# Norms of six attention heads and three SSD groups by sums in rows, a factor row that goes through DRAM, and a third weight set added up by GpSimd

## The chip, the cores and the metric

The kernel runs on one core of a Trainium2 chip. The metric is the device time of one execution in microseconds (us). A core has a matrix engine (TensorE, "PE" in the profile, its weight loads "PEld"), an elementwise engine (VectorE, "DVE"), an activation engine (ScalarE, "ACT"), a third elementwise engine (GpSimd, "POOL"), and SP, which only issues DMAs. Each engine works through its own list of instructions in order; semaphores hold an instruction back until what it reads is there.

## The reference

One layer of a hybrid decoder on 512 tokens of width 1024: a SwiGLU feed-forward part (FFN1), a mixer in which a Mamba-2 state-space part (SSD, 16 heads in 4 groups) and a differential attention (8 heads of width 128) share the input and the output projection, a cross-attention into 256 memory tokens, a second feed-forward part (FFN2), and norms before each. The two places whose norms the change touches:

```python
y = y.reshape(bsz, seqlen, SSD_WIDTH) * jax.nn.silu(z.astype(jnp.float32))
yg = y.reshape(bsz, seqlen, SSD_GROUPS, SSD_WIDTH // SSD_GROUPS)
yg = yg * lax.rsqrt(jnp.mean(yg * yg, axis=-1, keepdims=True) + EPS)
...
o = diff_attention(q, k, v, lam, rel_bias)
o = o * lax.rsqrt(jnp.mean(o * o, axis=-1, keepdims=True) + EPS)
y_attn = (o.astype(h.dtype) * subln_w * (1.0 - lambda_init)).reshape(bsz, seqlen, DA_WIDTH)
...
return jnp.concatenate([y_ssd, y_attn], axis=-1) @ w_out
```

Each attention head is normed over its 128 columns, each SSD group over its 256.

## The kernel before

Activations lie with the channel on the 128 partitions and the 512 tokens along the free axis, so a head's output `po` or half a group's output `y` is one 128x512 tile. Every fp32 product is done in three fp32r passes: an operand is split into a high part (`hi`, a rounded copy by ScalarE) and a low part (`lo`, the rest, a subtraction by VectorE), and high x high, high x low and low x high are added up in PSUM (`split`, `split_w`, `weights`, `proj`). Weights come by SP's DMA queue into `wr` tiles (six buffers), their two parts into `wh` and `wl` (three buffers each).

FFN1 and FFN2 save products in the manner of Strassen and Winograd: blocks of weights and of activations are added up first (`sums_in_steps` for the activations, sums `S1` to `S4`), and seven products stand in for eight. `out_blocks` is FFN's output product: `oa` = B11 x "11", `oe` = S1 x S1, `ob` = a copy of `oa` plus S2 x S2, then B21, S3, S4 and "22". `parts` are its two pairs of weight blocks. FFN1's last third runs it with `by_dma=True`: the sums of weights are made there, S1 and S3 by fetches that add on arrival (from GpSimd's DMA queue, `added`), S2 (the third set of weights, from `t_raw`) by adds of VectorE (`t2`, line 1366) of the blocks `more` that `ask_early` fetched. The generator stops once (`yield` behind `ready`), before the last activations are gated, and goes on when the products start.

The order of TensorE's work is written by a planner at build time. `Order` has a list of dense work (projections) and chains beside it (heads, groups, norms); a chain's `yield d` means "not before d us more of planned TensorE time", and while it waits the dense work is issued. The table `W` holds these times. On SP and GpSimd the written order stands; on the other engines the scheduler may move an instruction within its dependences, and `behind(...)` orders it.

A head (`head`): scores, softmax, transposes, `po`; then ScalarE copies `po` to `of`, four transposes to `ptk` put tokens on partitions, ScalarE squares them with an accumulator (`ss`), VectorE makes `ev`, GpSimd the power -1/2 (`rr`, line 858), VectorE multiplies (`on`, line 860), four transposes to `pot` turn it back, and the split into `ya` takes the gain `wsub` with it. `out_attn(0, ...)` and `out_attn(1, ...)` multiply heads 0 to 3 and 4 to 7 by their output weights (`pm`), and wait at build time until all four `ya` are there.

A group (`group`): at the end the two halves `yz` are squared and added, four products with a column of ones give the sums per token (`pn`), GpSimd takes the power, and `row_of` turns the factors into a row: two diagonal matrices `ndiag` (by GpSimd in groups 0 to 2, by VectorE in group 3), two products with ones (`nrow`); VectorE multiplies (line 1034) and `ys` is split. `out_proj` needs `ys` 0 to 5 first, and the last two (group 3) later.

All along, `block_sums_in_dram` adds up FFN2's weight blocks in DRAM: one fetch by SP and one accumulating DMA by GpSimd for each, of 512 KB mostly.

Of the kernel before, what the change touches and what calls it, by code (L numbers as in the profile page):

```python
# [11 lines left out]
F32 = mybir.dt.float32  # L12
# [5 lines left out]
P = 128  # L18
# [82 lines left out]
def body(tc, a, dbg=None):  # L101
# [25 lines left out]
    def small(s, n, bufs=None):  # L127
        return tiny.tile([P, n], F32, tag=s, name=nm(s), bufs=bufs)
# [15 lines left out]
    def mm(out, w, x, start, stop):  # L144
        od.t += (1 if w.dtype == R32 else 4) * (x.free_size() + 8) / 2400
        newest_mm[:] = [nc.tensor.matmul(out, w, x, start=start, stop=stop).ins]  # L146

    def transpose(out, x):
        od.t += 2 * (P + 8) / 2400
        nc.tensor.transpose(out, x, ident)  # L150
# [617 lines left out]
    def head(hd, q, kq, bias):  # L768
# [73 lines left out]
        w0.clear()  # L842
        w1.clear()
        of = s2("of")
        S.activation(of, po, AF.Copy)
# [8 lines left out]
        ev = small("ev", 4)  # L854
        V.scalar_tensor_tensor(ev, sm[0], EPS, sm[0], ALU.mult, ALU.mult)
        V.scalar_tensor_tensor(ev, ss, 1.0 / P, ev, ALU.mult, ALU.add)  # L856
        rr = small("rr", 4)
        G.tensor_tensor(rr, ev, mhalf, ALU.pow)  # L858
        on = s2("on", shape=(P, 4, P))
        V.tensor_tensor(on, pt.rearrange("p (a b) -> p a b", b=P), rr[:, :, None].to_broadcast([P, 4, P]), ALU.mult)  # L860
        yield W["hp"]
        pt = aux("pot")
        for b in range(4):
            transpose(pt[:, b * P : (b + 1) * P], on[:, b])
        ya[hd] = split("ya", backwards(pt), wsub)
        dump(f"ya_{hd}", ya[hd][0])

    wcv = []

# [60 lines left out]
    def group(g, bt, ct, xs, zs):  # L930
# [93 lines left out]
        yield W["gq"] + (1.2 if g == 2 else 0.0)  # L1024
        pn = aux("pn", (P, 4))
        for b in range(4):
            mm(pn[:, b : b + 1], sq[0][:, b * P : (b + 1) * P], ones[:, 0:1], True, True)

        rh = inv_rms_cols(pn, 4, 4.0 / (4 * 256), 4.0 * EPS)
        yield W["gn"]  # L1030
        pr = yield from row_of(rh, 4, *((G, G) if g < 3 else (V, V)), W["gr"] - (0.8 if g == 3 else 0.0))
        for j in range(2):
            n = 2 * g + j
            V.scalar_tensor_tensor(yz[j], yz[j], par[:, C_SSD + n : C_SSD + n + 1], pr, ALU.mult, ALU.mult)
            ys[n] = split("ys", yz[j])
            dump(f"ys_{n}", ys[n][0])


# [254 lines left out]
    def out_blocks(blocks, sums, g, col4, ncol4, each=None, finale=None, clean=True, n=None, by_dma=False):  # L1293
# [11 lines left out]
            nc.sync.dma_start(raw, of[:, part[0] * T : part[1] * T])  # L1305
            return raw

        def weights(of, part, raw=None, low_behind=()):
# [5 lines left out]
            high = S.activation(hi, raw, AF.Copy)  # L1314
            with behind(low_behind):
                low = V.tensor_tensor(lo, raw, hi.bitcast(F32), ALU.subtract)  # L1316
            recent[:] = [high.ins, low.ins]
            return hi, lo

        def some(ps, w, which, part, t, first, ks=None, passes=range(3)):  # L1320
# [39 lines left out]
            return t_raw[part]  # L1360

        def t2(part):
            more = pieces.pop(part) if part in pieces else (fetch(blocks[B22], part),)
            n = t_raw[part].shape[1] // len(more)
            for i, m in enumerate(more):
                V.tensor_tensor(t_raw[part][:, i * n : (i + 1) * n], t_raw[part][:, i * n : (i + 1) * n], m, ALU.add)
            return t_raw[part]

        def b21(part):
# [9 lines left out]
        later, pieces, asked = {}, {}, {}  # L1379

        def ask_early():
            for of, make in ((B11, lambda part: fetch(blocks[B11], part)), (S1, t1)):
                asked[of, parts[1]] = make(parts[1])
            for part in parts:
                pieces[part] = [s2("more") for _ in range(*part)]
                for k, m in zip(range(*part), pieces[part]):
                    nc.sync.dma_start(m, blocks[B22][:, k * T : (k + 1) * T])
# [28 lines left out]
        for m in both:  # L1416
            yield from m
        u2 = []
        third = {part: weights(sums[2], part, low_behind=() if n else sums_low) for n, part in enumerate(parts if by_dma else parts[:1])}
        third_split = list(recent) if by_dma else []  # L1420
        for t in range(2):
            S.activation(b_ps[t], a_ps[t], AF.Copy)
# [202 lines left out]
```

## Time and profile before

| | |
|---|---|
| median of 3 runs | 1295.64 us (1294.69 to 1296.42) |
| the profiled execution | 1296.8 us, span 1295.0 us |
| mean granted TensorE clock | 0.996 |
| POOL, busy | 116.4 us (9%) |
| DMA | 234.75 MB, mean 181 GB/s |

The span goes from the first to the last instruction; the time of an execution has a little more around it. A row of the chain of waits or of the timeline is "start us, us, engine, what". A group is "line engine operation out<-in, shapes xcount | busy us, mean ns | idle before, and what ended it". The stage in question of FFN1 lies from 300 to 343 us, the heads and groups from 385 to 805, FFN2 from 960 on.

### The profile page before, as it was taken

How to read it: one execution, taken by the hardware profiler on the slowest of the kernel's cores; microseconds unless marked ns; L12 is line 12 of the kernel's file. 1: busy time of each engine (PE TensorE's matmuls, PEld its weight loads, DVE VectorE, ACT ScalarE, POOL GpSimd, SP SyncE). 2: the span in 40 equal slices, each digit the busy share in tenths (PEclk: the TensorE clock that was granted, in tenths of full speed). 3: DMA queues.
4: the chain of work that ended last, by engine and by line, in shares of the span. 5: the costliest groups of instructions: out<-in, count | busy, mean ns of one | idle time of the engine just before them, and what ended most of it. 6: DMA issues, size and time to landing. Idle time of an engine off the chain costs nothing.

```text
span 1295.0 us, 20087 instructions
## 1 busy us (share of the span) xinstructions
PE 1282.7 (99%) x7709; PEld 1124.9 (87%) x7709; DVE 973.5 (75%) x1553; ACT 707.2 (55%) x1203; POOL 116.4 (9%) x145
## 2 busy tenths in 40 slices
PE   9999999999999999999999999999999999999997
PEld 7889998998888788877888888889899999989995
DVE  6988898797875776567778697645678878877886
ACT  7545564565654564346644575435466646555554
POOL 1001010001010011100102011020001000000000
PEclk9999999999999999999999999999999999999998
DMA  9368677889874436653475667593249876666662
GB/s 334 97 175 205 181 204 196 226 200 238 260 242 147 139 66 164 225 165 98 106 206 168 175 161 232 190 231 111 66 131 253 212 228 178 191 189 189 184 198 91
DMA packets 69551, 234.75 MB, mean 181 GB/s; under 512 B 8192, under 2 KB 9696, under 8 KB 69104
## 3 DMA queue, kind: packets, MB, share of 16 engines
q1 hardware_dynamic: 53488, 180.91, 42.5%
q0 software_dynamic: 13168, 45.67, 20.0%
q10 hardware_dynamic: 2800, 6.91, 1.6%
q8 instruction: 60, 0.98, 0.3%
q14 instruction: 35, 0.29, 0.1%
HBM read 231.30 MB, written 48.29 MB: 216 GB/s over the span
## 4 chain that ended last, share of the span: by engine, by line
PE 98%; DVE 1%; ACT 0%; issue 0%; POOLq 0%; POOL 0%; ACTq 0%
PE qb L243 13%; PE pm L146 10%; PE qe L243 8%; PE qa L243 8%; PE pxbc L146 7%; PE ob L1328 7%; PE oa L1328 4%; PE oe L1328 4%; PE pk L146 3%; PE pv L146 3%; PE pq L146 3%; PE pcq L146 3%; PE pz L146 3%; PE pck L146 2%; PE pa L146 2%; PE pcv L146 2%
## 5 line engine op out<-in xcount | busy, mean ns | idle before, releaser
L155 ACT ACTIVATE wh<-wr 128x1024 fp32r<-128x1024 f32 (+1 forms) x245 | 251.5, 1028 | 239.0 <-PE qe L243 29.4
L156 DVE TENSOR_TENSOR wl<-wr,wh 128x1024 fp32r<-128x1024 f32 (+1 forms) x245 | 291.1, 1189 | 78.3 <-ACT wh L155 57.8
L1314 ACT ACTIVATE wh<-wr 128x1024 fp32r<-128x1024 f32 (+1 forms) x78 | 77.1, 988 | 71.3 <-PE ob L1328 19.7
L1316 DVE TENSOR_TENSOR wl<-wr,wh 128x1024 fp32r<-128x1024 f32 (+1 forms) x78 | 87.6, 1131 | 15.1 <-ACT wh L1314 12.9
L790 ACT ACTIVATE ec<-ec,mn 128x512 f32<-128x512 f32 (+3 forms) x64 | 35.4, 554 | 21.9 <-DVE mn L789 21.9
L789 DVE CUSTOM_DVE_ANT_0 ec<-ps,bias 128x512 f32<-128x512 f32 (+3 forms) x64 | 28.1, 487 | 15.4 <-PE ps L146 15.3
L252 POOL DMA_DIRECT2D wr<-in_f2q x11 | 9.7, 881 | 308.8 <-DMA wr<-in_f2q 176.3
L367 POOL TENSOR_TENSOR ncol<-nv,mhalf 128x4 f32<-128x4 f32 (+1 forms) x9 | 10.6, 1179 | 295.3 <-DVE nv L365 295.3
L903 DVE SCALAR_TENSOR_TENSOR conv<-pxbc,par,conv 128x511 f32<-128x511 f32 (+2 forms) x48 | 35.8, 745 | 0.6
L146 PE MATMUL pxbc<-hnl,wh 128*128 128x512 f32 x128 | 35.5, 404 | 0.0
L146 PE MATMUL pxbc<-hnh,wh 128*128 128x512 f32 x128 | 34.7, 398 | 0.0
L146 PE MATMUL pxbc<-hnh,wl 128*128 128x512 f32 x128 | 32.5, 393 | 0.0
L454 DVE TENSOR_TENSOR gate<-qb,row 128x512 f32<-128x512 f32 x19 | 13.2, 692 | 22.1 <-PE qb L243 22.1
L146 PEld LDWEIGHTS pxbc<-hnh,wl 128*128 128x128 f32 x128 | 23.7, 188 | 5.2 <-issue 0.2
L252 POOL DMA_DIRECT2D wr<-in_f1q x16 | 14.0, 874 | 151.9 <-DMA wr<-in_f1q 83.0
L146 PEld LDWEIGHTS pxbc<-hnh,wh 128*128 128x128 f32 x128 | 23.3, 189 | 4.6 <-issue 0.3
L146 PEld LDWEIGHTS pxbc<-hnl,wh 128*128 128x128 f32 x128 | 23.2, 188 | 4.7 <-issue 0.4
L455 ACT ACTIVATE gate<-gate 128x1024 f32<-128x1024 f32 x19 | 20.1, 1056 | 10.9 <-DVE gate L454 10.9
L146 PE MATMUL pv<-wh,hnh 128*128 128x512 f32 x64 | 25.3, 396 | 0.0
L146 PE MATMUL pv<-wh,hnl 128*128 128x512 f32 x64 | 25.2, 393 | 0.0
L155 ACT ACTIVATE s24h<-s 128x512 fp32r<-128x512 f32 x30 | 18.8, 626 | 8.1 <-DVE s L214 8.1
L858 POOL TENSOR_TENSOR rr<-ev,mhalf 128x4 f32<-128x4 f32 x8 | 8.3, 1035 | 162.4 <-DVE ev L856 162.4
(465 smaller groups left out, 3548.1 us busy)
## 6 DMA issues: line engine op xcount, KB each, us to landing
wr<-in_f2q SPq DMA_DIRECT2D x44, 512.0 KB, 4.5
wr<-in_f1q SPq DMA_DIRECT2D x40, 512.0 KB, 4.6
wr<-in_f1b SPq DMA_DIRECT2D x23, 512.0 KB, 7.0
isum<-in_f2q SPq DMA_DIRECT2D x22, 512.0 KB, 5.2
wr<-isum SPq DMA_DIRECT2D x22, 512.0 KB, 6.2
wsum<-in_f2b SPq DMA_DIRECT2D x20, 512.0 KB, 6.1
wr<-wsum SPq DMA_DIRECT2D x20, 512.0 KB, 4.7
wr<-in_f1q POOLq DMA_DIRECT2D x16, 512.0 KB, 7.6
```

The source lines that it names most:

```text
L146: newest_mm[:] = [nc.tensor.matmul(out, w, x, start=start, stop=stop).ins]
L155: S.activation(hi, src, AF.Copy),
L156: V.tensor_tensor(lo, src, hi.bitcast(F32), ALU.subtract),
L243: newest_mm[:] = [nc.tensor.matmul(out, w_[:, wc], xs[kp][which][x_], start=first and j == 0 and f == 0 and kp == 0, stop=j == 2 and kp == ...
L252: last_sum[:] = [G.dma_start(raw, m, accum_op=ALU.add).ins]
L455: S.activation(gate, gate, AF.Silu)
L789: V.tensor_tensor_reduce(out=ec[:, :n], in0=ps[c][:, parts[i]], in1=bias[:, T - n :], scale=0.125, scalar=3e38, op0=ALU.add, op1=ALU.min, ...
L790: S.activation(ec[:, :n], ec[:, :n], AF.Exp, bias=mn, scale=-1.0, accum_out=sm[c][:, i : i + 1])
L903: V.scalar_tensor_tensor(y[:, d:], ps[:, : T - d], par[:, cw + j : cw + j + 1], y[:, d:], ALU.mult, ALU.add)
L1314: high = S.activation(hi, raw, AF.Copy)
L1316: low = V.tensor_tensor(lo, raw, hi.bitcast(F32), ALU.subtract)
L1328: newest_mm[:] = [nc.tensor.matmul(ps, a_[:, ts], b_[:, ws], start=first and k == 0 and j == 0, stop=k == n - 1 and j == 2, skip_group_che ...
```

## The change

There are three edits. (1) Heads with `hd % 4 < 3`, six of eight: `po` is squared by ScalarE, the squares are split, and two products with ones (`sums_by_token`, `ptok`) put the sum over the channels into every partition; VectorE takes the diagonal of each 128x128 block with `tensor_tensor_reduce`, which gives a column per token. The factors go to DRAM as a column and come back as a row on all partitions (`row_by_dram`, two DMAs of GpSimd), and GpSimd multiplies, copies and subtracts (`times_row`), so that the parts of `ya` need no transposes. Heads 3 and 7 keep the old way (`by_token`). (2) Groups 0 to 2 the same with `ys`; the gain is taken by ScalarE beforehand; group 3 keeps the old way. (3) In FFN1's last third the adds of the third weight set go to GpSimd (`add_pieces`); `ask_early` is called before the stop, S3's fetches are asked for later and part by part, the second part of B11 is split behind the first block's parts (`first_block`), and the third set's high part is made before the products, its low part after them.

```diff
+W |= {"hn": 4.2, "fw": 5.0, "fr": 16.0}
...
+    def sums_by_token(sq):
+
+        ps = aux("ptok")
+        with behind(list(newest_mm)):
+            for j in range(2):
+                mm(ps, ones_r, sq[j], j == 0, j == 1)
+        ss = small("ss", 4)
+        junk = s2("junk", shape=(P, P))
+        for b in range(4):
+            V.tensor_tensor_reduce(out=junk, in0=ps[:, b * P : (b + 1) * P], in1=ident, scale=1.0, scalar=0.0, op0=ALU.mult, op1=ALU.add, accum_out=ss[:, b : b + 1])
+        return ss
+
+    def row_by_dram(col):
+        there = dram.tile([4, P], F32, name=nm("there"))
+        G.dma_start(bass.AP(there.tensor, there.offset, [[1, P], [P, 4]]), col)
+        yield W["fw"]
+        row = s2("far")
+        G.dma_start(row, bass.AP(there.tensor, there.offset, [[0, P], [1, 4 * P]]))
+        yield W["fr"]
+        return row
+
+    def times_row(src, row, seen=lambda t: t):
+
+        hi, lo = s2("farh", R32), s2("farl", R32)
+        G.tensor_tensor(src, src, row, ALU.mult)
+        G.tensor_copy(hi, seen(src))
+        G.tensor_tensor(lo, seen(src), hi.bitcast(F32), ALU.subtract)
+        return hi, lo
...
-        S.activation(of, po, AF.Copy)
-        yield W["hv"]
-        pt = aux("ptk")
+        if hd % 4 < 3:
+            sq = s2("osq")
+            S.activation(sq, po, AF.Square)
+            S.activation(of, po, AF.Copy, scale=wsub)
+            sq = split("osq", sq)
+            yield W["hn"]
+            ss = sums_by_token(sq)
+        else:
+            S.activation(of, po, AF.Copy)
+            yield W["hv"]
+            pt = aux("ptk")
+            ss = by_token(pt, of)
...
+        if hd % 4 < 3:
+            row = yield from row_by_dram(rr)
+            ya[hd] = times_row(of, row, backwards)
...
+        gains = [par[:, C_SSD + 2 * g + j : C_SSD + 2 * g + j + 1] for j in range(2)]
+        if g < 3:
+            sq = split("ysq", sq[0])
+            for j in range(2):
+                S.activation(yz[j], yz[j], AF.Copy, scale=gains[j])
+            yield W["gq"] + (1.2 if g == 2 else 0.0)
+            row = yield from row_by_dram(inv_rms_cols(sums_by_token(sq), 4, 4.0 / (4 * 256), 4.0 * EPS))
...
+            if g < 3:
+                ys[n] = times_row(yz[j], row)
...
         def t2(part):
-            more = pieces.pop(part) if part in pieces else (fetch(blocks[B22], part),)
-            n = t_raw[part].shape[1] // len(more)
-            for i, m in enumerate(more):
-                V.tensor_tensor(t_raw[part][:, i * n : (i + 1) * n], t_raw[part][:, i * n : (i + 1) * n], m, ALU.add)
+            V.tensor_tensor(t_raw[part], t_raw[part], fetch(blocks[B22], part), ALU.add)
             return t_raw[part]
...
-            for part in parts:
-                asked[S3, part] = seventh(part)
+            add_pieces(parts[0])
+
+        def add_pieces(part):
+            for i, more in enumerate(pieces.pop(part)):
+                to = t_raw[part][:, i * T : (i + 1) * T]
+                G.tensor_tensor(to, to, more, ALU.add)
...
             ready = [{parts[0]: weights(of, parts[0])} for of in (blocks[B11], sums[0])]
+            if by_dma:
+                ask_early()
             yield
         if by_dma:
-            ask_early()
+            asked[S3, parts[0]] = seventh(parts[0])
+            ready[0][parts[1]] = weights(None, parts[1], asked.pop((B11, parts[1])), first_block)
+            with behind(first_block[:1]):
+                third[parts[0]] = weights(None, parts[0], t_raw[parts[0]], low=False)
+            copied_behind = [recent[0]]
...
-        third = {part: weights(sums[2], part, low_behind=() if n else sums_low) for n, part in enumerate(parts if by_dma else parts[:1])}
-        third_split = list(recent) if by_dma else []
-        for t in range(2):
-            S.activation(b_ps[t], a_ps[t], AF.Copy)
-        with behind(third_split):
+        if by_dma:
+            V.tensor_tensor(third[parts[0]][1], t_raw[parts[0]], third[parts[0]][0].bitcast(F32), ALU.subtract)
+            add_pieces(parts[1])
+            asked[S3, parts[1]] = seventh(parts[1])
+        else:
+            third[parts[0]] = weights(sums[2], parts[0], low_behind=sums_low)
+        with behind(copied_behind):
+            copied = [S.activation(b_ps[t], a_ps[t], AF.Copy).ins for t in range(2)]
+        if by_dma:
+            with behind(copied):
+                third[parts[1]] = weights(None, parts[1], t_raw[parts[1]])
+        with behind(list(recent) if by_dma else []):
             for t in range(2):
                 update(t + 2, 1, e_ps[t], 1, False)
```

More of the change, by code (lines that the diff above doesn't have):

```diff
@@ L844, in head, with by_token @@
         of = s2("of")
-        S.activation(of, po, AF.Copy)
-        yield W["hv"]
-        pt = aux("ptk")
+        if hd % 4 < 3:
[10 more added lines that the diff above has]
+            ss = by_token(pt, of)
+        ev = small("ev", 4)
+        V.scalar_tensor_tensor(ev, sm[0], EPS, sm[0], ALU.mult, ALU.mult)
+        V.scalar_tensor_tensor(ev, ss, 1.0 / P, ev, ALU.mult, ALU.add)
+        rr = small("rr", 4)
+        G.tensor_tensor(rr, ev, mhalf, ALU.pow)
+        if hd % 4 < 3:
+            row = yield from row_by_dram(rr)
+            ya[hd] = times_row(of, row, backwards)
+        else:
+            on = s2("on", shape=(P, 4, P))
+            V.tensor_tensor(on, pt.rearrange("p (a b) -> p a b", b=P), rr[:, :, None].to_broadcast([P, 4, P]), ALU.mult)
+            yield W["hp"]
+            pt = aux("pot")
+            for b in range(4):
+                transpose(pt[:, b * P : (b + 1) * P], on[:, b])
+            ya[hd] = split("ya", backwards(pt), wsub)
+        dump(f"ya_{hd}", ya[hd][0])
+    def by_token(pt, of):
         for b in range(4):
@@ L853, in head @@
             S.activation(junk, pt[:, b * P : (b + 1) * P], AF.Square, accum_out=ss[:, b : b + 1])
[L854 to L866, printed above, removed]
+        return ss
     wcv = []
@@ L1023, in group @@
         V.tensor_tensor(sq[0], sq[0], sq[1], ALU.add)
[L1024 to L1031, printed above, removed]
+        gains = [par[:, C_SSD + 2 * g + j : C_SSD + 2 * g + j + 1] for j in range(2)]
[5 more added lines that the diff above has]
+            row = yield from row_by_dram(inv_rms_cols(sums_by_token(sq), 4, 4.0 / (4 * 256), 4.0 * EPS))
+        else:
+            yield W["gq"]
+            pn = aux("pn", (P, 4))
+            for b in range(4):
+                mm(pn[:, b : b + 1], sq[0][:, b * P : (b + 1) * P], ones[:, 0:1], True, True)
+            rh = inv_rms_cols(pn, 4, 4.0 / (4 * 256), 4.0 * EPS)
+            yield W["gn"]
+            pr = yield from row_of(rh, 4, V, V, W["gr"] - 0.8)
         for j in range(2):
             n = 2 * g + j
-            V.scalar_tensor_tensor(yz[j], yz[j], par[:, C_SSD + n : C_SSD + n + 1], pr, ALU.mult, ALU.mult)
-            ys[n] = split("ys", yz[j])
+            if g < 3:
+                ys[n] = times_row(yz[j], row)
+            else:
+                V.scalar_tensor_tensor(yz[j], yz[j], gains[j], pr, ALU.mult, ALU.mult)
+                ys[n] = split("ys", yz[j])
             dump(f"ys_{n}", ys[n][0])
@@ L1306, in fetch, with weights @@
             return raw
-        def weights(of, part, raw=None, low_behind=()):
+        def weights(of, part, raw=None, low_behind=(), low=True):
             if raw is None:
@@ L1314, in weights @@
             high = S.activation(hi, raw, AF.Copy)
+            recent[:] = [high.ins]
             with behind(low_behind):
-                low = V.tensor_tensor(lo, raw, hi.bitcast(F32), ALU.subtract)
-            recent[:] = [high.ins, low.ins]
+                if low:
+                    recent.append(V.tensor_tensor(lo, raw, hi.bitcast(F32), ALU.subtract).ins)
             return hi, lo
@@ L1377, in t4 @@
             G.dma_start(t_raw[part], blocks[B21][:, part[0] * T : part[1] * T], accum_op=ALU.add)
-        later, pieces, asked = {}, {}, {}
+        later, pieces, asked, third, copied_behind = {}, {}, {}, {}, []
         def ask_early():
```

1 line of the change is left out of this document (added).

## The prediction

> **What bounds the kernel now.** I read the page first (busy time, chain by engine), then the waits of TensorE, then the timeline and the chain of waits where TensorE waits longest, then the groups of the tiles that the diff removes.
>
> ```profile
> span 1295.0 us, 20087 instructions
> PE 1282.7 (99%) x7709; PEld 1124.9 (87%) x7709; DVE 973.5 (75%) x1553; ACT 707.2 (55%) x1203; POOL 116.4 (9%) x145
> ...
> PE 98%; DVE 1%; ACT 0%; issue 0%; POOLq 0%; POOL 0%; ACTq 0%
> ```
>
> The waits of TensorE and of its weight loads (us in total, times, longest):
>
> ```profile
> PE ob L1328 <- ACT wh L1314: 1.1, 1, 1.1
> ...
> PEld ptk L150 <- ACT of L845: 0.9, 4, 0.3
> ...
> PEld pot L150 <- DVE on L860: 0.4, 2, 0.2
> ...
> PEld oe L1328 <- DVE s31l L156: 0.2, 1, 0.2
> ```
>
> TensorE is busy 99% and is 98% of the chain that ended last. So the end moves for two reasons only: instructions leave TensorE's stream, or one of its few waits goes or comes. After the start-up the longest wait is one in front of `ob`, the S2 product at the end of FFN1. The timeline around it (start, us, what), then the chain of waits, then busy us of TensorE, its weight loads, VectorE, ScalarE and GpSimd in stretches of 1 us, with the granted clock behind them:
>
> ```profile
> 310.27 0.69 DVE L156 TENSOR_TENSOR s24l<-s,s24h 128x512 fp32r<-128x512 f32 x1
> ...
> 310.88 0.69 DVE L156 TENSOR_TENSOR gl<-th,gh 128x512 fp32r<-128x512 f32 x1
> 311.48 2.49 DVE L1366 TENSOR_TENSOR wr<-wr,more 128x512 f32<-128x512 f32 x4
> ...
> 311.82 1.03 PE L146 MATMUL prel<-hot,rel_sb 32*8 32x256 f32 x4
> ...
> 312.86 2.27 ACT L1314 ACTIVATE wh<-wr 128x1024 fp32r<-128x1024 f32 x2 [1.14 <-DVE wr L1366]
> ```
>
> ```profile
> 313.97 7.33 PE ob L1328 x24
> 321.31 5.44 PE oa L1328 x24
> ```
>
> ```profile
> 312.00:313.00 1.00, 0.85 (x4) 0.17 (x2) 1.00 (x3) 0.14 (x1) 0.79 (x1) 1.00 0.99 397
> 313.00:314.00 1.00, 0.03 (x1) 0.03 (x1) 1.00 (x3) 0.92 (x1) 0.00 (x0) 1.00 1.03 406
> ...
> 315.00:316.00 1.00, 1.00 (x3) 0.78 (x3) 1.00 (x2) 1.00 (x5) 0.52 (x1) 0.50 0.98 352
> ```
>
> The third set of weights (S2's) is made last: VectorE finishes the blocks' low parts, only then adds `more` into it, then ScalarE splits it. TensorE idles 0.15 + 0.97 = 1.1 us. Then the granted clock falls to 0.50, and the 24 products take 7.33 us where the next 24 take 5.44: another 1.9 us. The unit price of a 512-column product is 5.44 / 24 = 0.227 us.
>
> The Trainium skill ("TensorE: Matmul & The Clock Gate", What's actually happening) puts the fall to half speed after an idle window of about 3.4 us. Here it followed 1.1 us of idleness behind the four small `prel` products; by that page alone the gap costs 1.1 us and not 3.0, and the sum below would be -5.2 instead of -7.1; the measured clock decides.
>
> **The change, part by part.** *Six heads.* The path of TensorE loses eight 128x128 transposes a head and gets two 512-column products with ones.
>
> ```profile
> 467.32 1.90 PE po L146 x12
> ...
> 470.78 0.44 PE ptk L150 x4
> ...
> 478.18 0.44 PE pot L150 x4
> ...
> 486.96 0.44 PE ptk L150 x4
> ```
>
> That is 0.44 + 0.44 - 2 x 0.227 = 0.43 us a head, 2.6 us for six. The waits of `ptk` and `pot` (0.9 and 0.4 us over eight heads) go with them, about 1.0 for six. In their place the sums wait for a longer line: Square, copy with gain, high part (ScalarE), low part (VectorE), instead of one copy; the plan gives it 4.2 instead of 2.08 us. I cost the old waits and the new ones as equal, 0, between -1.0 (none left) and +1.8 (the longest old one, 0.3, at all six). The scores and transposes of other heads and the dense products stand between, so TensorE waits only for what arrives late.
>
> Behind the sums nothing of these heads is on TensorE: four diagonal products (VectorE), `ev`, the power on GpSimd, a DMA to DRAM, one back to all partitions, and three 128x512 passes on GpSimd.
>
> ```profile
> L858 POOL TENSOR_TENSOR rr<-ev,mhalf 128x4 f32<-128x4 f32 x8 | 8.3, 1035 | 162.4 <-DVE ev L856 162.4
> ...
> L698 POOL TENSOR_TENSOR ea<-euler,hb 128x16 f32<-128x16 f32 x1 | 2.9, 2923 | 6.1 <-DMA hb<-in_hb 6.1
> ...
> L789 DVE CUSTOM_DVE_ANT_0 ec<-ps,bias 128x128 f32<-128x128 f32 x16 | 4.0, 286 | 0.0
> L860 DVE TENSOR_TENSOR on<-ptk,rr x8: 691/692/692, 420.9 to 647.6; 128x512 f32<-128x512 f32 x8
> L160 DVE SCALAR_TENSOR_TENSOR yal<-pot,wsub,yah 128x512 fp32r<-128x512 f32 x8 | 6.0, 748 | 3.7 <-ACT yah L159 3.5
> 385.00:505.00 120.00, 119.97 (x635) 95.77 (x634) 82.12 (x216) 64.49 (x163) 12.29 (x14) 1.00 0.47 123
> ```
>
> VectorE loses `on` and `yal` (0.69 + 0.75) and gets the low part of the squares and four diagonals (0.69 + 4 x 0.29 = 1.83): +0.4 us a head, in a stretch where it is busy 82 of 120 us; hidden. ScalarE, busy 64 of 120, loses four squares with accumulators and a split, and gets two passes. GpSimd gets three passes and two DMA issues, at 12 busy us of 120. Two of the passes read the block backwards, which no row shows on GpSimd; I bound a pass between 0.69 us (VectorE's for a block of that size) and 2.9 (GpSimd's longest, `ea`) and take 1.03, that of `ndiag` (quoted below), the row of equal size and engine.
>
> *Does the row come in time?* Head 2 is the last with the new norm ahead of the output product.
>
> ```profile
> L146 PEld LDWEIGHTS pm<-yah,wh x64: 186/188/190, 504.2 to 763.6; 128*128 128x128 f32 x64
> ...
> cum_d<-ct_sb POOLq DMA_DIRECT2D x1, 32.0 KB, 2.5
> ...
> hb<-in_hb POOLq DMA_DIRECT2D x1, 16.0 KB, 7.0
> ...
> isum<-in_f2q POOLq DMA_DIRECT2D x1, 512.0 KB, 13.7
> ```
>
> Its `po` ends at 469.2; with 4.2 planned the sums run at 473.5 and end at 474; 1.2 (diagonals), 0.3 (`ev`), 1.0 (power) and 0.9 (issue) give 477.4. The first reader of `ya` is at 504.2, the passes take 3.1, so both DMAs together have 504.2 - 3.1 - 477.4 = 23.7 us. I bound one by 2.5 us (the small write of `cum_d`) and 13.7 (the slowest block sum on that queue, since these stand before them in it): 5 to 27 us, and take 2 x 7.0, the small load `hb` on the same queue, the nearest to the broadcast. So 10 us are left: cost 0, and at the upper end 3.7 us late. The 512 scattered words of the write are in no row; the same bounds serve. While GpSimd waits to issue the read, block sums and the next head's power queue behind it. Head 3's `ptk` is at 487.0 and its power comes after, so a write that lands within 10 us of 477.4 delays nobody; one that lands later holds `on` of head 3 and then its `pot`. SP's queue is not passed by any of these; its fetches of block sums merely find their adders later.
>
> *Three groups.* TensorE loses `pn` (four fp32 products) and `nrow`, and gets two products:
>
> ```profile
> 541.78 0.79 PE pn L146 x8
> ...
> 549.31 0.46 PE nrow L146 x2
> L146 PEld LDWEIGHTS pm<-ysh,wh x64: 186/188/189, 793.3 to 834.7; 128*128 128x128 f32 x64
> 756.52 0.79 PE pn L146 x8
> ```
>
> 0.79 + 0.46 - 0.45 = 0.80 us each, 2.4 us for three. The results are needed from 793.3 on; group 2, the last, has its sums at 756.5 and has 36.8 us for 7 us of instructions, 3.1 us of further passes and two DMAs: hidden. Group 3, which really ends late, keeps its old norm.
>
> *The third set.* The adds go to GpSimd, the first part's before the blocks are made, its high part in front of the products, its low part behind them. Then nothing of VectorE's line lies ahead of `ob` except `s24` (ready at 311.0), so up to 1.1 us of idleness and 1.9 us of slow clock go, plus 0.2 that `oe` waits for `s31l` (the last row of the waits above): 3.2 at most.
>
> ```profile
> 294.10 1.75 SPq L1387 DMA_DIRECT2D more<-in_f1b  x4
> ...
> 311.91 0.88 POOL L1354 DMA_DIRECT2D gate<-in_f1b  x1 [6.59 <-ACT ob L1422]
> ```
>
> The fetches that move with it (B11 and S1 of the second part, S1's accumulating one on GpSimd, four `more`) keep their order on SP, which held `more` to 294.1; their earlier place gains and costs 0. On GpSimd the second part's adds now stand before S3's accumulating fetch, issued at 311.9 today. S3 is read after `oa`, at 321.3 + 5.4 = 326.7, or 3 us sooner; 2.1 us of adds leave it 9.7 us. I cost that at 0; at the slowest row, 13.7, it would be 4 us.
>
> Below, the gain is bounded by nothing, and by a loss if the adds hold up VectorE, for which this trace has a row:
>
> ```profile
> 702.81 1.03 POOL L378 TENSOR_TENSOR ndiag<-ident,cl 128x512 fp32r<-128x512 f32 x1
> ...
> 703.05 1.87 DVE L156 TENSOR_TENSOR wl<-wr,wh 128x1024 fp32r<-128x1024 f32 x1 [0.41 <-PE pxbc L146]
> L156 DVE TENSOR_TENSOR wl<-wr,wh 128x1024 fp32r<-128x1024 f32 x229 | 280.1, 1224 | 77.2 <-ACT wh L155 57.8 <-PE pv L146 5.0 <-PE pxbc L146 4.0
> ```
>
> A low part that takes 1.22 us took 1.87 beside the GpSimd pass: 0.65 lost, as if it had started only when that pass ended at 703.84. VectorE is fully busy in all three windows above, and the second part's two adds fall on `s31l` and `s24l`, two-input operations like that one. So I leave about 0.65 of the 1.1 idle us standing, count the 0.2 as kept, and let the clock recover: 0.5 + 1.9 = 2.4 us gained, between -1.3 (two such losses and no gain, slower) and 3.2.
>
> The Trainium skill ("SBUF — State Buffer", two separate sides) makes this a rule: GpSimd and a VectorE operation with two SBUF inputs exclude each other for a whole instruction. The trace agrees with its 1.87 us; by the rule alone the adds free nothing on VectorE, since four passes of 1.03 us lock out more than the 2.5 us that they took there; with the clock's 1.9 us alone left of the third set the sum would be -6.6.
>
> In the mixer 36 such passes come and six `ndiag` passes go. Each burst of three can push one low part by 0.65: 12 bursts, 0 to 7.8 us. Behind 703.05 TensorE did not wait, and VectorE has a third of its time free; I take 0.3.
>
> **The sum**: -2.6 (heads) - 2.4 (groups) - 2.4 (third set) + 0.3 = -7.1 us. The profiled execution took 1296.8 us (1.8 around its span), so 1289.7; the median of the runs, 1295.64, is 1.2 below it: **1288.5 us**.
>
> **Rivals.** (a) *The third set is still what ends last*: its raw part, the copies of `oa` or the locked-out low parts arrive no earlier, the gap and the slow clock stay, and only 2.6 + 2.4 - 0.3 = 4.7 us come: 1290.9. For it: VectorE had no free time there. Against: the high part, the wait that ended last, no longer stands behind VectorE. Here the change would not do what it says.
>
> (b) *The lock reaches TensorE*: every burst costs its 0.65, and the third set gains only 2: -2.6 - 2.4 - 2.0 + 7.8 = +0.8, no change, 1296.4. For it: 703.05. Against: low parts are made a set or more ahead.
>
> (c) *The row comes late, slower than before*: it decides from the point where write and read of heads 2 and 6 take over 23.7 us together. At 13.7 each TensorE waits 3.7 us at both attention output products, and pays 1.9 of slow clock each time: +11.2 - 7.1 = +4.1, 1299.7. For it: the read waits in GpSimd's line, behind block sums in the same queue. Against: 10 us of room.
>
> **How the numbers follow.** Forecast 0.60 (1286 to 1290.5); (a) 0.19 (1290.5 to 1293); (b) 0.12 (1293 to 1298); (c) 0.06; 0.03 for a larger gain, where no new wait takes the place of the 1.0 at the transposes and the third set yields 3.2 (1286 and below). A measurement of this kernel can tell about 0.2% from no change, 2.6 us. Faster by that, under 1293.05: the forecast, (a), the larger gain and a little of (b), 0.83; within it, most of (b): 0.10; slower: (c) and an end of (b): 0.07. The range 1285.3 to 1293.5 takes in the forecast's bounds (1.9 more at best) and (a), and leaves out under 2 in 10.
>
> **What would show it.** Right: in six heads two `ptok` products of some 0.45 us together where eight transposes took 0.88; no clock of 0.50 between 312 and 320 and 5.4 us for `ob`; `pm` not waiting for `ya`. Wrong: a wait of `pm` on GpSimd or a DMA (c); low parts over 1.8 us with TensorE waiting behind them (b); a window at 0.50 still there (a). Waits of the new products for the low part of the squares over 0.3 us would make the heads' step wrong.

## The result, and the profile after

| | before | changed |
|---|---|---|
| median | 1294.69 us (1293.2 to 1296.42, 5 runs) | 1309.11 us (1306.51 to 1310.17, 5 runs) |
| profiled execution, span | 1296.8, 1295.0 us | 1309.11, 1307.3 us |

The ratio is 1.0109, with a 95% interval of 1.0098 to 1.012: slower by 14 us, where 7 us faster was forecast. The page of the changed kernel (span, busy time, chain by engine):

```profile
span 1307.3 us, 20098 instructions
PE 1285.3 (98%) x7649; PEld 1122.9 (86%) x7649; DVE 976.2 (75%) x1606; ACT 703.6 (54%) x1164; POOL 168.4 (13%) x191
PE 93%; DVE 3%; DMA 2%; issue 1%; ACT 1%; POOL 0%; POOLq 0%; DVEq 0%; ACTq 0%
```

60 matmuls have left the stream, yet TensorE is busy longer: it ran part of them at a lower clock. Its waits (us in total, times, longest):

```profile
PE pn L147 <- DVE ysq L1069: 4.4, 1, 4.4
PE ptok L147 <- ACT osqh L156: 4.2, 1, 4.2
PE pf L147 <- DVE st L1024: 1.9, 2, 1.5
...
PE py L147 <- DVE gate L1041: 1.1, 1, 1.1
PE oe L1385 <- DVE s31l L157: 0.9, 1, 0.9
```

Apart from `oe`, they lie in three places, around 625, 735 and 800 us, and the granted clock falls in each (windows of the changed kernel; the number before the two last columns is the clock):

```profile
620.00:625.00 5.00, 2.59 (x14) 1.64 (x12) 0.70 (x2) 0.70 (x2) 3.15 (x4) 1.00 0.31 46
625.00:630.00 5.00, 3.10 (x15) 1.91 (x16) 4.79 (x13) 3.67 (x10) 1.39 (x2) 0.72 0.62 100
630.00:635.00 5.00, 5.00 (x18) 3.93 (x19) 4.97 (x26) 3.36 (x11) 1.87 (x2) 0.59 0.26 69
...
735.00:740.00 5.00, 3.89 (x22) 3.08 (x22) 5.00 (x9) 2.77 (x5) 0.26 (x1) 0.66 1.03 236
...
805.00:810.00 5.00, 4.97 (x12) 3.54 (x13) 1.67 (x4) 0.00 (x0) 4.86 (x6) 0.50 0.71 296
```

**Head 6** (timeline of the changed kernel; in brackets the idle time before and what ended it):

```profile
612.81 0.83 POOL L385 DMA_DIRECT2D there<-rr  x1 [0.96 <-POOL rr L891]
621.68 0.55 POOL L388 DMA_DIRECT2D far<-there  x1 [8.05 <-PE pxbc L147]
622.25 1.28 POOL L395 TENSOR_TENSOR of<-of,far 128x512 f32<-128x512 f32 x1
...
623.56 0.69 DVE L819 CUSTOM_DVE_ANT_0 ec<-ps,bias 128x512 f32<-128x512 f32 x1 [6.62 <-POOL of L395]
...
626.06 0.63 ACT L156 ACTIVATE osqh<-osq 128x512 fp32r<-128x512 f32 x1
...
626.74 0.50 PE L147 MATMUL ptok<-osqh,ones_r 128*128 128x512 f32 x1 [4.15 <-ACT osqh L156]
```

GpSimd issues head 5's write at 612.8 and stands 8 us in front of head 5's read. (By the trace the write lands at 621.1, and the read starts 0.6 us later, as each of the nine reads does behind its write; the releaser named there is that of another semaphore.) Behind the read in its list stands head 4's multiplication, whose row is there. VectorE's `ec` of the next softmax gets the tile that this multiplication gives back, so it waits 6.6 us, ScalarE's squares stand behind it, and TensorE behind those.

**The memory tiles** of the cross-attention come by GpSimd's queue too, and now stand behind group 1's read:

```profile
705.67 0.86 POOL L385 DMA_DIRECT2D there<-ncol  x1 [0.30 <-POOL ncol L368]
...
716.79 0.59 POOL L388 DMA_DIRECT2D far<-there  x1 [9.35 <-DMA there<-ncol]
717.91 3.05 POOL L1100 DMA_DIRECT2D mem<-in_memT  x5
...
729.49 0.51 ACT L160 ACTIVATE hm<-mem,par 128x256 fp32r<-128x256 f32 x1 [5.69 <-DMA mem<-in_memT]
...
731.20 2.31 DVE L157 TENSOR_TENSOR wl<-wr,wh 128x1024 fp32r<-128x1024 f32 x1
...
733.90 0.49 PE L147 MATMUL pf<-th,st 128*128 128x128 f32 x2 [1.46 <-DVE st L1024]
```

Before, these loads were issued from 705.0 on:

```profile
L1044 POOL DMA_DIRECT2D mem<-in_memT x8: 538/1136/1192, 705.0 to 713.2; - x8
```

The low part `wl`, ahead of the `st` that `pf` waits for, takes 2.31 us beside a pass of GpSimd (731.07 to 732.42), where such low parts take 1.22.

**Groups 2 and 3**, ahead of the output projection:

```profile
780.29 0.86 POOL L385 DMA_DIRECT2D there<-ncol  x1 [0.30 <-POOL ncol L368]
...
793.95 0.59 POOL L388 DMA_DIRECT2D far<-there  x1 [12.79 <-PE pcv L147]
...
801.22 2.20 POOL L395 TENSOR_TENSOR y<-y,far 128x512 f32<-128x512 f32 x1 [5.75 <-DMA far<-there]
802.21 1.75 DVE L1069 TENSOR_TENSOR ysq<-ysq,ysq 128x512 f32<-128x512 f32 x1
...
804.11 1.28 PE L147 MATMUL pn<-ones,ysq 128*128 128x1 f32 x8 [4.40 <-DVE ysq L1069]
```

The first `pm` needs group 2's parts, which GpSimd makes from 801 on. Before, eight of these products lay ahead of group 3's `pn`; now nothing is left to run ahead of it. And `ysq`, which `pn` waits for, takes 1.75 us beside GpSimd's pass, where its neighbours of that size take 0.69.

The common part is the write. Issues of the changed kernel (KB each, median us to landing):

```profile
far<-there POOLq DMA_DIRECT2D x9, 256.0 KB, 7.1
...
there<-rr POOLq DMA_DIRECT2D x6, 2.0 KB, 10.1
...
there<-ncol POOLq DMA_DIRECT2D x3, 2.0 KB, 10.9
```

2 KB take over 10 us, longer than the 256 KB of the row, and GpSimd stands in front of all nine reads.

### The profile page after: what moved, and what is told of

It is laid out like the page before. It is cut to its first block, busy times and chain, and to the rows that moved or that the text cites. A ratio compares the mean times of both kernels' runs of the same rounds, so it can differ in the third digit from the quotient of the medians.

```text
span 1307.3 us, 20098 instructions
## 1 busy us (share of the span) xinstructions
PE 1285.3 (98%) x7649; PEld 1122.9 (86%) x7649; DVE 976.2 (75%) x1606; ACT 703.6 (54%) x1164; POOL 168.4 (13%) x191
## 4 chain that ended last, share of the span: by engine, by line
PE 93%; DVE 3%; DMA 2%; issue 1%; ACT 1%; POOL 0%; POOLq 0%; DVEq 0%; ACTq 0%
PE qb L244 13%; PE pm L147 10%; PE qe L244 8%; PE qa L244 8%; PE ob L1385 6%; PE pxbc L147 5%; PE oa L1385 4%; PE oe L1385 4%; PE pk L147 3%; PE pq L147 3%; PE pv L147 3%; PE pcq L147 3%; PE pz L147 3%; PE pck L147 2%; PE pa L147 2%; PE pg L147 2%
## 5 line engine op out<-in xcount | busy, mean ns | idle before, releaser
L147 PE MATMUL pm<-farh,wh 128*128 128x512 f32 x96 | 29.0, 419 | 0.3 <-DVE x L923 0.2
L147 PE MATMUL pm<-farl,wh 128*128 128x512 f32 x96 | 27.5, 407 | 0.0
L147 PE MATMUL pm<-farh,wl 128*128 128x512 f32 x96 | 26.8, 398 | 0.0
```

## Experiments

Theory 1: the slow write holds GpSimd's list in front of each read, and what stands behind it, or waits for a tile it frees, comes late. Rivals: the added passes lock VectorE out; the row itself is late; the new order of TensorE's work is to blame. For each kernel this table gives how much later (+) TensorE starts the same products than in the profile of before, in us, worked out from the start times of both timelines (medians over stretches of before's time, minus the same difference at 340 to 400 us, which leaves start-up and FFN1 out). Head 6 lies between the first two columns, the memory tiles and the output projection between the last two.

```
                          585-612   680-715   840-1000
changed kernel             -2.0      +4.5      +16.1
e1 third set alone          0.0       0.0        0.0
e2 heads alone             -0.1      +8.9       +8.9
e3 groups alone            -0.8      -0.8      +14.6
e4 row from a constant     -2.1      +1.1       +5.1
e5 read 14 behind write    -2.0      -1.1       +8.5
e7 memory loads by SP      -1.8      +3.4      +12.3
e8 group 2 old             -1.9      +5.4       +6.8
e9 write in 128 pieces     -1.7      -2.4       +6.1
e11 e5 and e8              -1.4      +2.8       +7.2
e12 e9's write and e8      -1.5      -2.2       -0.5
e13 e9's write, short plan -1.9      +0.9       +6.8
e15 row in its own tiles   -0.5      +7.1      +22.2
e16 e12, multiplying only  +0.5      +1.7       +1.9
e17 e12, low part twice    -0.4      -0.6       +0.7
e18 e12 without third set  -1.6      -2.2       -0.5
```

### Each edit alone

e1 is the kernel before with the edits of FFN1's last third; e2 with `head`'s, `sums_by_token`, `row_by_dram` and `times_row`; e3 with `group`'s and these helpers.

> The kernel before with the third weight set's edit alone. Every theory here has this edit as a gain: oa started 1.9 us earlier in the changed kernel. Expected 1292.5 us (1291.8 to 1293.3), 2 us under before. If instead it is level with before, the 1.9 us are given back later in the span.

> The kernel before with the six heads' edit alone. Theory 1 (GpSimd's queue is held by the wait for the scattered write, and what stands behind it is late): -2.6 for the products, +7 for the wait of ptok on osqh at head 6 with the slow clock behind it: 1299 us, with that wait of over 3 us in TensorE's waits. Theory 2 (the 18 added GpSimd passes lock VectorE out): low parts late, 1294 to 1298, no single wait over 2 us. Theory 3 (the two edits of the norms only hurt together, through one another's passes and tiles): 1292.

> The kernel before with the three groups' edit alone. Theory 1: -2.4 for the products, +4 at the memory tiles that group 1's waiting read delays, +9 at group 3's pn: 1305 us, with mem tiles issued about 13 us later than before. Theory 2 (lock): 1295 to 1299, with ysq and wl long and the mem tiles on time. Theory 3: 1292.

Measured: e1 1294.56 us, ratio 1.0005 (0.9996 to 1.0015); e2 1301.35, 1.0057 (1.0042 to 1.0072); e3 1308.72, 1.0114 (1.0099 to 1.0129). e2 and e3 show theory 1's waits, somewhat dearer than expected (`ptok` on `osqh` 7.1 us in e2). The two losses do not add up: in the last column 8.9 and 14.6 stand against 16.1 together. e1 is a miss: no gain. It was not given back later either, as the table shows. The reason is in e2, which has FFN1 as before (timeline, then windows):

```profile
312.65 1.19 PE L1374 MATMUL ob<-wh,s24h 128*128 128x512 f32 x4 [0.97 <-ACT wh L1360]
```

```profile
313.00:314.00 1.00, 1.00 (x6) 0.82 (x5) 1.00 (x2) 1.00 (x2) 0.00 (x0) 1.00 0.79 193
...
315.00:316.00 1.00, 1.00 (x6) 0.80 (x6) 1.00 (x3) 0.91 (x2) 0.65 (x3) 1.00 1.10 258
```

The same wait in front of `ob` as before, and the clock stays at 1.00. So does it in e3 (1.13 us of waiting) and e18 (0.7). The mean granted clock says the same: 0.996 in the profiled execution of before, 0.997 or 0.998 in the 75 later ones on record. So the 1.9 us at 0.50 belonged to that one execution, not to the kernel. And the wait itself is only moved, as e1's timeline shows:

```profile
308.92 3.08 POOL L1391 TENSOR_TENSOR wr<-wr,more 128x512 f32<-128x512 f32 x2 [2.75 <-DVE wl L1318]
...
310.92 0.72 PE L1329 MATMUL oe<-wh,s31l 128*128 128x512 f32 x2 [0.96 <-DVE s31l L156]
```

GpSimd's two adds take 1.54 us each beside VectorE, `s31l` comes late by as much as `wh` did, and TensorE waits 0.96 us one product earlier.

### The write, and who waits for it

e4 takes the wait away by other data, e5 plans the read later, e9 makes the write faster:

```diff
 e4
-        G.dma_start(row, bass.AP(there.tensor, there.offset, [[0, P], [1, 4 * P]]))
+        G.dma_start(row, a["final"][0].partition_broadcast(P))
 e5
-W |= {"hn": 4.2, "fw": 5.0, "fr": 16.0}
+W |= {"hn": 4.2, "fw": 14.0, "fr": 9.0}
 e9
-        G.dma_start(bass.AP(there.tensor, there.offset, [[1, P], [P, 4]]), col)
+        G.dma_start(bass.AP(there.tensor, there.offset, [[4, P], [1, 4]]), col)
```

> The changed kernel in full, but the broadcast read takes a fixed row of the final gain in DRAM in place of the row just written: the write is still issued, nobody waits for it, and the heads' and groups' norm factors are left out of the result. GpSimd's passes, their number and TensorE's instructions stay. Theory 1 (the wait for the write): all three stalls go, 1288 to 1291 us. Theory 2 (lock by 36 passes): they stay, 1303 to 1309. Theory 3 (the new order of TensorE and VectorE around group 3): the waits of ptok at head 6 and of the memory tiles go, the wait of pn stays: 1297 to 1300.

> The changed kernel with one number moved: the read of the row is planned 14 us behind the write instead of 5 (and the passes 9 us behind the read instead of 16, so nearly the same 23 us in all). The write took 9 to 14 us to be done in the changed kernel. Theory 1 (what costs is that GpSimd stands in front of the read, and everything behind it in its list with it): the read finds its row there, GpSimd does not stand, and the time comes down to about that of the fixed row, 1296 to 1300 us. Rival (the row itself comes too late for its readers): the row comes no sooner, so 1307 to 1312.

> The changed kernel, but the factors are written to DRAM as they lie, 16 bytes from each partition in one piece (128 pieces), not as 512 single words; the row is read as before, so the factors stand in another order of tokens in the result. If the number of single words sets how long the write takes, it is done in 3 to 5 us instead of 9 to 14 and the time is near that of the fixed row, 1296 to 1300. If the write's time is that of any small write of this queue behind the block sums, it stays at 9 us or more and 1305 to 1310.

Measured: e4 1297.49 us, 1.0028 (1.0016 to 1.004): theory 1's 1288 to 1291 was missed and theory 3's range met, with 1.3 us of `pn`'s wait left; e5 1299.26, 1.0029 (1.0018 to 1.004); e9 1299.2 in one run. Each takes 10 to 12 of the 14 us away without taking a pass or a product away, so most of the loss comes from the read's wait for its write and from what stands behind it. e5 met its number, but not for the reason expected: GpSimd still stands. Eight of its nine reads start right after their write has landed, six of them after more than 8 us of idleness. What changed is the list, where head 4's multiplication now comes before head 5's read (timeline of e5):

```profile
612.45 0.83 POOL L385 DMA_DIRECT2D there<-rr  x1 [0.96 <-POOL rr L891]
614.38 1.27 POOL L395 TENSOR_TENSOR of<-of,far 128x512 f32<-128x512 f32 x1 [1.11 <-DMA far<-there]
...
622.20 0.59 POOL L388 DMA_DIRECT2D far<-there  x1 [3.65 <-DVE wl L157]
```

So it is what stands behind the wait that costs, more than the wait. In e4 the rows still came late, which fits a read that stands in the queue behind its write (issue to landing of `far` in e4, where the changed kernel has 7.1):

```profile
DMA to landing us min/median/max: 10.6/14.9/17.2
```

e9 shows what makes the write slow (its issues):

```profile
there<-rr POOLq DMA_DIRECT2D x6, 2.0 KB, 2.9
...
there<-ncol POOLq DMA_DIRECT2D x3, 2.0 KB, 2.9
```

The same 2 KB from the same queue, in 128 pieces instead of 512: 2.9 us instead of 10.1. At 700 us e5 and e9 are still 1.1 and 2.4 us ahead of before; they lose it, and more, at groups 2 and 3. In e5 `pm` waits there for group 2's parts themselves:

```profile
793.65 0.50 PE L147 MATMUL pm<-farh,wh 128*128 128x512 f32 x1 [3.38 <-POOL farh L396]
796.89 0.79 PE L147 MATMUL pm<-farh,wh 128*128 128x512 f32 x1 [2.74 <-POOL farh L396]
```

### The places behind the wait

e7 loads the memory tiles by SP, e8 norms group 2 the old way, e15 gives the row tiles of its own:

```diff
 e7
-            od.spawn(memory_prep(hm2, 3.0, 4, nc.gpsimd), 1.0)
+            od.spawn(memory_prep(hm2, 3.0, 4, nc.sync), 1.0)
 e8 (in both places of group)
-        if g < 3:
+        if g < 2:
 e15
-        row = s2("far")
+        row = sp.tile([P, T], F32, tag="far", name=nm("far"), bufs=2)
...
-NHALF = 16
+NHALF = 12
```

> The changed kernel, but the memory tiles are loaded through SP's list instead of GpSimd's. If they were late because their loads stood behind group 1's read, which waited 9.4 us for its write, they come on time, pf and py no longer wait behind hm, and some 4 us go: 1304 to 1306 us; head 6 and group 3 stay as they were. If VectorE is late there because of GpSimd's passes, it stays at 1308 to 1311.

> The changed kernel with group 2 normed in the old way; groups 0 and 1 and the six heads stay new. If group 2's late sums, its waiting read and its passes beside group 3's squares are what made pn wait 4.4 us with the slow clock behind it, that stall (7 to 10 us) goes and 0.8 of products come back: 1299 to 1302 us, with no wait of pn over 1 us. If the new order of TensorE around group 3 is to blame, whatever group 2 does, it stays at 1308 to 1311.

> The changed kernel, but the row gets two tiles of its own instead of a slot of the common pool (paid for with four fewer half-size slots). If the wait at head 6 comes over a slot (VectorE's ec writes where the row of head 4 lay, which GpSimd reads late), VectorE no longer waits for GpSimd there, ptok starts on time and some 7 us go: 1301 to 1303 us, with the stalls at the memory tiles and at group 3 as they were. If VectorE is late there for another reason, 1307 to 1311.

Measured: e7 1306.18 us, 1.0091 (1.0077 to 1.0105); e8 1299.89, 1.004 (1.0025 to 1.0055); e15 1312.9, 1.0135 (1.0114 to 1.0157). e7 takes 3 us away, at the edge of what was expected, and `pf` and `py` no longer wait: the memory tiles were late by their place in the list. (`pxbc` now waits 1.7 us for weights, which come by SP too.) e8 takes 9 away, and `pn`'s wait is gone, with head 6's still there (5.3 us). e15 is a miss; its timeline shows why:

```profile
618.59 0.69 DVE L819 CUSTOM_DVE_ANT_0 ec<-ps,bias 128x512 f32<-128x512 f32 x1
...
629.65 0.69 ACT L878 ACTIVATE of<-po,wsub 128x512 f32<-128x512 f32 x1 [7.46 <-POOL farl L397]
...
630.90 0.79 PE L147 MATMUL ptok<-osqh,ones_r 128*128 128x512 f32 x1 [6.58 <-ACT osqh L156]
```

`ec` no longer waits, as expected. But now ScalarE's `of` writes where GpSimd's late pass still reads, waits 7.5 us, and `osqh` stands behind it. (The half-size slots that e15 gives up do not hold `of`.) It is not one tile: whatever GpSimd frees late, the next user of the common pool waits for.

### The passes themselves

e10 is e4 with VectorE and ScalarE doing `times_row`. e16 and e17 start from e12 (below): e16 leaves GpSimd the multiplication only, e17 makes its low part twice.

```diff
 e10
-        G.tensor_tensor(src, src, row, ALU.mult)
...
+        V.tensor_tensor(src, src, row, ALU.mult)
+        return split("far", seen(src))
 e16
...
-        G.tensor_copy(hi, seen(src))
-        G.tensor_tensor(lo, seen(src), hi.bitcast(F32), ALU.subtract)
-        return hi, lo
+        return split("far", seen(src))
 e17
         G.tensor_tensor(lo, seen(src), hi.bitcast(F32), ALU.subtract)
+        G.tensor_tensor(lo, seen(src), hi.bitcast(F32), ALU.subtract)
```

> The kernel with the fixed row in place of the written one (1297.5 us; norm factors left out), with the three passes of times_row taken from GpSimd: VectorE multiplies and makes the low part, ScalarE the high part. Theory of the lock (what is left above before is VectorE standing while GpSimd's 36 passes of 0.6 to 1.3 us run): 1290 to 1293. Rival (what is left is the new order of TensorE's and VectorE's work, above all pn of group 3 ahead of pm): 1296 to 1299.

> The short write with group 2 old (1292.3 us), with GpSimd doing only the multiplication; ScalarE makes the high part and VectorE the low part. GpSimd loses 20 passes (some 19 us), VectorE gets 10 of 0.7 us. Theory of the lock: VectorE is late less often, 1290 to 1291.5. Rival (an instruction on VectorE or ScalarE that waits for GpSimd's product holds all that stands behind it): 1294 to 1300, with a wait of VectorE on GpSimd in the list.

> The short write with group 2 old (1292.3 us), with GpSimd's last pass, the low part, made twice: 10 passes of 1.3 us more beside VectorE, nothing else changed. Theory of the lock at the prediction's price (up to 0.65 a pass, when TensorE waits for each): up to 6.5 us, 1294 to 1299. Rival (VectorE's spare time swallows them): 1291.5 to 1293.5, no difference.

Measured: e10 1373.03 us, 1.0608 (1.0592 to 1.0624); e16 1294.86, 1.0003 (0.9994 to 1.0012); e17 1292.53, 0.9983 (0.9974 to 0.9992), against e12's 1292.33. Ten more passes of GpSimd cost nothing that can be measured (0.2 us, give or take about 1), and 20 fewer, handed to the others, cost 2.5 us: ScalarE's `farh` then waits 16.0 us for GpSimd's product, and `po` 2.6 us for ScalarE. So the lock is hardly what is left. e10, which was far outside both theories, shows what the place of a wait is worth (VectorE's waits):

```profile
DVE of L394 <- DMA far<-in_final: 57.5, 6, 13.4
...
DVE y L394 <- DMA far<-in_final: 31.2, 3, 11.6
```

The same late rows, waited for by an engine with three quarters of its time in use instead of one with an eighth: 89 us, and 75 of them on the end. e10 therefore says nothing of the lock.

### Versions

e11 is e5 with e8. e12 is e8 with e9's write and a multiplication that reads the row in the order in which it then lies; e13 has all three groups, e12's write and a shorter plan; e18 is e12 without the edits of FFN1.

```diff
 e12
-W |= {"hn": 4.2, "fw": 5.0, "fr": 16.0}
+W |= {"hn": 4.2, "fw": 6.0, "fr": 15.0}
...
-        G.tensor_tensor(src, src, row, ALU.mult)
+        by = src.rearrange("q (b p) -> q b p", b=4)
+        G.tensor_tensor(by, by, row.rearrange("q (p b) -> q b p", b=4), ALU.mult)
```

> Both cures together: the read planned 14 us behind the write, and group 2 normed in the old way. With the longer wait alone TensorE stood 4 us ahead of before until 790 us of the span and lost 11 at group 2's row; with group 2 old and the short wait it lost 7 at head 6. If these are separate places, both go: six heads at 0.43 and two groups at 0.80 remain, -4.2 from before's 1294.5: 1289.5 to 1291.5 us. If the 30 passes left on GpSimd cost VectorE something, 1292 to 1295.

> The changed kernel with group 2 old, the write in 128 pieces of 16 bytes instead of 512 words, and GpSimd's multiplication reading the row in that order (steps of 16 bytes), so that the result is whole. The short write took 5 us to the next issue instead of 9 to 14. Expected as for the planned longer wait with group 2 old: 1289.5 to 1291.5 us. If reading the row in steps makes the multiplication slower than 1.3 us or the shorter chain does not matter once nobody waits, 1291 to 1295.

> All three groups and six heads new, the write in 128 pieces, and the plan told so: 6 us to the read, 8 to the passes (14 in all instead of 21). If the stall at group 2 and 3 comes from the planned 21 us, which let the dense work run out ahead of out_proj, it goes: 1288.5 to 1291 us. If it comes from the real time of group 2's sums, row and passes (27 us), it stays in part: 1295 to 1300, with pn or pm waiting over 2 us around 795.

> The short write with group 2 old (1292.3 us), without the third weight set's edit. Alone that edit gave 1.0005 of before. If it is worth nothing, 1291.5 to 1293; if its moved wait costs or gains up to 1 us here, 1291 to 1294. In its profile ob waits about 1.1 us for ScalarE's wh with the clock at 1.00 behind it; a clock of 0.50 there would bring the old theory back.

Measured: e11 1296.12 us (1293.46 to 1300.34), 1.0012 (1.0001 to 1.0022); e12 1292.33, 0.9982 (0.9974 to 0.9991); e13 1299.69, 1.0041 (1.0026 to 1.0055); e18 1292.08, 0.9976 (0.9967 to 0.9986). e12 and e18 are 2 us faster than before. In the profiles most of that lies behind TensorE's last product: against e1, which has the same FFN1, e12's profiled span is 2.3 us shorter, and only 0.7 of it up to the last product. e11 missed both ranges. In its profiled execution, the slowest (1300.3 us), head 4's row landed 13.7 us behind its read, and `ptok` waited 2.8 us; the faster ones have no profile, so its spread stays open. e13 shows that group 2 does not fit in the new way even with the fast write and a shorter plan; `pm` waits for VectorE's `cvl` (2.2 us) and `py` for its masks (3.3). Some 3 of its 7 us, though, are lost ahead of group 2, as the second column shows. Whether the planned or the real lateness does it is not settled, since the shorter plan moved other work together too. The longest of e12's waits of TensorE that are not start-up:

```profile
PE pst L147 <- DVE xde L1000: 1.0, 1, 1.0
PE oe L1386 <- DVE s31l L157: 1.0, 1, 1.0
PE pxt L151 <- DVE th L935: 0.9, 2, 0.5
PE pt L151 <- DVE ec L832: 0.7, 2, 0.4
```

Apart from FFN1's `oe`, 2.6 us of waits on VectorE remain. By the table e12 is 0.5 us ahead at the output projection instead of 4.2. These waits are most of the rest; e17 speaks against the lock, and what else makes VectorE late there was not found.

## Why the prediction was wrong

*Products of heads and groups, -2.6 and -2.4: right in price.* By 600 us three heads and one group had moved TensorE 2.0 us ahead; 3 x 0.43 + 0.80 is 2.1.

*Third set, -2.4: wrong, 0.* 1.9 of the 3.2 was a slow clock seen in one execution. That execution (1296.8) stood 2.1 us above the median, which the prediction had noticed (1.2 then) and put into the base, not into the term. The Trainium skill ("TensorE: Matmul & The Clock Gate", What's actually happening) puts the fall to half clock after an idle window of about 3.4 us. The falls behind 4.2 and 4.4 us of waiting here agree with that. Others do not: the clock also fell to 0.50 behind waits of 1.46 and 1.11 us at 732 to 736 us here, and behind 1.95 and 1.29 in e4, while it held behind 0.97 and 1.13 in front of `ob`, 2.25 in e13 and 2.78 in e11. So a gap of 1 to 3 us may or may not slow the clock, and no run shows what decides. The rest, 1.1, was traded for `oe`'s 0.96: the gap stayed nearly whole, where the prediction had left 0.65 of it standing. So rival (a) was right about the gap, not about the clock.

*Lock in the mixer, +0.3: too low, but not what failed.* Twice in the changed kernel a row of VectorE that is stretched beside GpSimd's passes stands right ahead of a wait of TensorE, as rival (b) asked: `wl` at 731.2 (1.1 us longer than usual) ahead of `pf`, and `ysq` at 802.2 (1.1 longer) ahead of `pn`. That is at most 2.2 of the 14 us. In e17 ten further passes cost nothing that can be measured, so the price that (b) put on every burst is out.

*The row through DRAM, "in time", cost 0: the step that failed.* Its sizes were inside the bounds (a write of 10.1 us between 2.5 and 13.7), and `pm` of the heads never waited for a row, so rival (c) failed at the place that it named. Wrong was "a write that lands within 10 us of 477.4 delays nobody". The prediction asked who waits behind the read for head 2 only, found head 3's power and the block sums, and let that answer stand for nine reads. For head 2 it nearly held: the read stood until 486.2, `on` of head 3 waited 3.0 us for its power, and `pot` not at all (0.8 us in e2). Behind head 5's read stood head 4's passes, and with them tiles of the common pool that VectorE and ScalarE needed; behind group 1's, the loads of the memory tiles, which the prediction did not see at all. e4, e5 and e9 show the size together, e7 the loads alone, e15 the tiles. The new waits of `ptok`, set between -1.0 and +1.8, came to 4.2 for that reason.

*Group 2, "hidden" in 36.8 us: wrong.* The prediction counted 10 us of work and two DMAs. The sums' products ran at 765, but the last of VectorE's diagonals only at 777.2; the write was issued at 780.3, the read at 794.0, the first pass at 801.2. Every step stood in somebody's line. e8 shows the place (9 us); the order in which TensorE ran out of dense work follows from it in the timeline, but was not tested alone.

*The account.* 16.1 us later at the output projection, less 1.6 at the end of FFN1, where before had its slow clock, 0.3 of start-up, and 2.0 behind the last product, is 12.2, and the profiled spans differ by 12.3.

## What to carry to other kernels

A DMA that waits for another DMA, on an engine that works its list in order, is priced by everything behind it in that list: passes, other loads, and the pool's tiles that these passes give back. Ask it at every place where the pair stands, and let the wait stand on the engine with the emptiest list, behind whatever others need from that list. Few pieces instead of many single words shorten the wait itself. And a slow clock seen in one profile is not a term of a sum before a second run shows it.

## What was not expected

- Scattering 2 KB as 512 words took 10.1 us to landing, as 128 pieces of 16 bytes 2.9. The Trainium skill ("DMA: Bandwidth & Descriptors", Anatomy of one DMA) gives a DMA about 2.0 us plus its bytes: near the second, far from the first. As an estimate from the two, a word more costs (10.1 - 2.9) / 384, or 19 ns.
- GpSimd's 128x512 passes took 1.28 us with two inputs and 0.61 as a cast in most rows of the changed kernel; reading backwards cost nothing extra. Reading the row in steps of 16 bytes, a multiplication took 1.55 (e12).
- From the start of TensorE's last product the span went on for 9.9 us in before's profile, 8.8 to 10.3 in e1 to e3, and 8.0 in the changed kernel and all kernels from e4 on. The last computing instruction ends within 0.3 us of the same place in all of them. What differs is the closing part: GpSimd's closing drain ends 8.5 to 9.1 us behind the last product in before, e1 and e3, where it ends the span, and 4.2 to 6.2 us behind it in the others. No run explains this. It gives 1.7 of the 2.3 us by which e12's profiled span is shorter than e1's.
